# A two-block layer network on one core: the modulation products moved from TensorE to VectorE, half of them into the first feed-forward, and the filter adds from GpSimd to VectorE

## The chip, the cores and the metric

The kernel runs on one core of one Trainium2 chip. The metric is the device time of one execution in microseconds; lower is better. A core has a matrix engine (TensorE, "PE" in the rows, its weight loads "PEld"), a vector engine (VectorE, "DVE"), a scalar engine (ScalarE, "ACT"), GpSimd ("POOL") and a queue engine (SyncE, "SP") from which most transfers are issued.

## The reference, cut to what matters

Two hybrid layers (512 tokens, width 1024) are followed by two conditioned layers. A conditioned layer needs a modulation: six rows of 1024 numbers for the tokens and six for a 256-token context, each a product of a vector with a weight matrix of 1024 x 6144.

```python
mod_x = (jax.nn.silu(c) @ w_mod[i] + b_mod[i])[:, None, :]
mod_c = (jax.nn.silu(c_ctx) @ w_mod[i] + b_mod[i])[None, None, :]
sh1, sc1, ga1, sh2, sc2, ga2 = jnp.split(mod_x, 6, axis=-1)
csh1, csc1, cga1, csh2, csc2, cga2 = jnp.split(mod_c, 6, axis=-1)
hx = rmsnorm_2(x, g_pre_mix[i]) * (1.0 + sc1) + sh1
...
x = x + ga1 * rmsnorm_2(mix_x, g_post_mix[i])
if not last:
    ...        # the context's own mixer and feed-forward
fx = rmsnorm_2(x, g_pre_ffn[i]) * (1.0 + sc2) + sh2
x = x + ga2 * rmsnorm_2(conv_ffn(fx, ...), g_post_ffn[i])
```

In the last layer the context only gives keys and values, so of its six rows only the first two (csh1, csc1) are used. Each conditioned layer also has a long convolution whose filter is made by a small network of sines and then normalised by its sum of absolute values.

## The kernel before, in words

`block1` computes the two hybrid layers, `block2` the two conditioned layers. Everything is unrolled. Large products are done in three parts (`mm3`, L560 to L562) on weights that are first split in two (`split`: ScalarE rounds, L528, VectorE subtracts, L529).

The order of the work is written out by generators. `weave` takes several generators with a total each, and always advances the one that has done the smallest share of its total (a `yield` of 0.45 adds 0.45). For each hybrid layer `weave_hybrid` weaves the attention, the dense products (`mtile`: a 512 KB weight tile, 24 matmuls) and side streams: the modulation and, in layer 0, the filters (`prep`). The order on an engine is then settled when the program is built, from the order of the code and from the dependences, so an instruction may stand ahead of earlier code that is not ready.

The modulation (`modulation`) loops over 2 layers, 6 rows and 8 blocks of 128 input features, 96 steps in all. A step loads 128 x 1024 weights (512 KB), multiplies them on TensorE in four column groups of 256 by the two activated vectors (L1322; a profile shows each as two matmuls, 8 to a step) and adds the bank to a 128 x 256 accumulator on VectorE (L1324 for the first block, L1326 for the others). After 8 steps come bias and gain (L1331, L1332) and the way out to DRAM. Layer 0's 48 steps are woven into hybrid layer 0, layer 1's into hybrid layer 1. `mod_columns` and `mod_row` read the rows back later.

`filters` runs three times beside hybrid layer 0. For each block of 128 positions it multiplies (L1217), decays (L1218), takes the absolute value (L1219), adds it to a total on GpSimd (L1221), and after the last block adds the halves on GpSimd (L1222), sums over partitions on TensorE (L1224), takes the reciprocal (L1225), makes sums and differences on GpSimd (L1231) and scales them (L1232). All the blocks of a call are issued in one step.

`Ffn.run` is the feed-forward. For conditioned layer 0 (tokens and context together, 768 columns) it makes 22 hidden tiles by `up` and takes them in ten parts of mostly two; for each part but the last, `down` is called six times (4 token tiles, 2 context tiles), each time for two banks of 512 columns, which VectorE adds to an accumulator (L2077; the first part is copied by ScalarE). `down` takes its banks from a ring of four, `up` from a ring of two pairs.

Of the kernel before, what the change touches and what calls it, by code (L numbers as in the profile page):

```python
# [11 lines left out]
AF = mybir.ActivationFunctionType  # L12
# [4 lines left out]
P = 128  # L17
# [254 lines left out]
def drain(gen):  # L272
    for _ in gen:
        pass
# [156 lines left out]
class Net:  # L431
# [273 lines left out]
    def block1(self):  # L705
# [32 lines left out]
        for l in range(DEPTH):  # L738
            self.weave_hybrid(l, [(self.some(mod, T["modn"] if l == 0 else 96), T[f"m{l}"])] + ([(self.some(prep, T["prepn"]), T["p0"])] if l == 0 else [(prep, T["p1"])]))
# [464 lines left out]
    def filters(self, l, tag, banks):  # L1204
# [7 lines left out]
        for t in range(nt):  # L1212
# [85 lines left out]
    def modulation(self):  # L1298
# [7 lines left out]
        cs = self.new(KD, 32)  # L1306
        nc.vector.memset(cs, 0.0)
        nc.vector.tensor_scalar(cs[:, :, 0:2], t.rearrange("p (s k) -> p k s", s=2), 0.5, None, op0=ALU.mult)
        self.mod = {}
        ws, accs = self.ring(1024, 2), self.ring(256, 2)  # L1310
        yield 0.0
        for l in range(DEPTH):
            md = self.dram(f"mod_{l}", (2, 6 * D))
            self.mod[l] = md
            for r in range(6):
                acc = accs()
# [12 lines left out]
                w = ws(512)  # L1329
                nc.sync.dma_start(w, d["modbg"][l, r])  # L1330
# [897 lines left out]
```

## Time and profile before

| | |
|---|---|
| median of 3 runs | 2293.55 us (2291.92 to 2294.4) |
| the profiled execution, its own time | 2299.32 us |
| its span, first to last instruction | 2297.3 us, 31229 instructions |
| PE busy | 2193.8 us, 95% |
| DVE busy | 1418.7 us, 62% |
| ACT busy | 1015.2 us, 44% |
| POOL busy | 231.6 us, 10% |
| mean granted TensorE clock | 0.985 of 2.4 GHz |
| moved by DMA | 235.88 MB, mean 103 GB/s |

An engine's busy time is the union of its instructions' durations. The ends of matmuls are modelled, so a PE that is busy all the time need not be at its peak. The span is read in stages: hybrid layer 0 is woven from about 65 to 330 us, hybrid layer 1 from about 420 to 665 us, the main part of the first feed-forward lies at 1110 to 1610 us.

### The profile page before, as it was taken

Reading aid. Unit: us, or ns where it says so; the run is one execution under the profiler, and the core shown is the slowest. Engines: PE = TensorE matmul, PEld = TensorE weight load, DVE = VectorE, ACT = ScalarE, POOL = GpSimd, SP = SyncE. Lnnn points to the kernel's source line nnn. Section 1 sums busy time; section 2 is a strip of 40 time slices with the busy share of each in tenths; the row PEclk is TensorE's granted clock in tenths of the full one; section 3 lists DMA queues with packets and bytes.
Section 4 is the critical chain, followed back from the end, with each engine's and each line's share of the span. In section 5 each row is a group of like instructions: output and inputs, shape, how many; then the busy total and the mean of one; then the engine's idle time right before and its main releaser. Section 6 shows DMA issues by size and latency. Waiting matters only on the chain.

```text
span 2297.3 us, 31229 instructions
## 1 busy us (share of the span) xinstructions
PE 2193.8 (95%) x12119; PEld 1748.6 (76%) x12122; DVE 1418.7 (62%) x2498; ACT 1015.2 (44%) x1896; POOL 231.6 (10%) x388
## 2 busy tenths in 40 slices
PE   7989999999999988999999999999899999999997
PEld 6545678755577777788888888888677889888886
DVE  5665776347667466676655655665877666456556
ACT  4335355246336335765532332323455664333332
POOL 2052012112012110010000000000320000000001
PEclk9989999999999999999999999999999999999999
DMA  5566523355532122323211221212134131233321
GB/s 193 176 193 197 180 78 106 116 178 169 166 114 74 46 76 98 112 77 111 83 56 46 83 74 55 70 60 67 49 101 135 60 102 65 74 101 110 101 93 63
DMA packets 72596, 235.88 MB, mean 103 GB/s; under 512 B 9056, under 2 KB 11136, under 8 KB 72448
## 3 DMA queue, kind: packets, MB, share of 16 engines
q1 hardware_dynamic: 65392, 223.06, 30.0%
q10 hardware_dynamic: 7056, 10.83, 1.6%
q8 instruction: 95, 1.56, 0.3%
q14 instruction: 53, 0.43, 0.1%
HBM read 225.37 MB, written 8.49 MB: 102 GB/s over the span
## 4 chain that ended last, share of the span: by engine, by line
PE 61%; DVE 6%; ACT 3%; POOL 3%; DMA 2%; issue 1%; POOLq 0%; DVEq 0%; ACTq 0%
PE f L561 10%; PE f L560 10%; PE f L562 10%; PE b L560 8%; PE b L562 7%; PE b L561 7%; POOL small L570 2%; PE b L1942 2%; PE b L909 2%; DVE page L529 1%; PE f L1915 1%; PE b L908 1%; ACT page L528 1%; PE f L1916 1%; POOL small L569 1%
## 5 line engine op out<-in xcount | busy, mean ns | idle before, releaser
L528 ACT ACTIVATE page<-page 128x1024 fp32r<-128x1024 f32 (+7 forms) x472 | 393.4, 846 | 639.8 <-PE f L561 159.5
L529 DVE TENSOR_TENSOR page<-page,page 128x1024 fp32r<-128x1024 f32 (+7 forms) x472 | 452.4, 970 | 319.4 <-ACT page L528 295.7
L560 PE MATMUL f<-page,page 128*128 128x512 f32 (+2 forms) x1452 | 518.0, 359 | 7.5 <-ACT page L528 7.5
L561 PE MATMUL f<-page,page 128*128 128x512 f32 (+2 forms) x1444 | 518.3, 359 | 1.0 <-DVE page L529 1.0
L560 PE MATMUL b<-page,page 128*128 128x512 f32 (+3 forms) x1356 | 513.0, 379 | 5.3 <-ACT page L528 1.7
L562 PE MATMUL f<-page,page 128*128 128x512 f32 (+2 forms) x1452 | 516.8, 357 | 0.0
L561 PE MATMUL b<-page,page 128*128 128x512 f32 (+3 forms) x1354 | 501.4, 371 | 0.4 <-DVE page L529 0.4
L562 PE MATMUL b<-page,page 128*128 128x512 f32 (+3 forms) x1346 | 498.3, 371 | 2.2 <-DVE page L529 2.2
L560 PEld LDWEIGHTS f<-page,page 128*128 128x128 f32 x1452 | 273.5, 189 | 51.3 <-ACT page L528 10.8
L560 PEld LDWEIGHTS b<-page,page 128*128 128x128 f32 x1356 | 256.1, 189 | 66.0 <-issue 16.4
L562 PEld LDWEIGHTS f<-page,page 128*128 128x128 f32 x1452 | 273.8, 189 | 39.8 <-DVE page L529 1.5
L561 PEld LDWEIGHTS f<-page,page 128*128 128x128 f32 x1444 | 272.8, 189 | 40.0 <-DVE page L529 3.1
L561 PEld LDWEIGHTS b<-page,page 128*128 128x128 f32 x1354 | 256.4, 189 | 47.9 <-issue 9.3
L562 PEld LDWEIGHTS b<-page,page 128*128 128x128 f32 x1346 | 254.7, 189 | 45.9 <-issue 5.6
L2077 DVE TENSOR_TENSOR page<-b,page 128x512 f32<-128x512 f32 x148 | 100.5, 687 | 84.5 <-PE b L562 84.4
L1401 ACT ACTIVATE page<-f,page 128x512 f32<-128x512 f32 (+1 forms) x128 | 89.2, 697 | 119.0 <-PE f L562 118.8
L569 POOL TENSOR_SCALAR small<-small 128x1 f32<-128x1 f32 (+3 forms) x104 | 41.8, 402 | 866.0 <-DVE small L2088 359.1
L1402 DVE SCALAR_TENSOR_TENSOR page<-f,page,page 128x511 f32<-128x511 f32 (+1 forms) x128 | 84.0, 656 | 69.8 <-ACT page L1401 69.7
L1403 DVE SCALAR_TENSOR_TENSOR page<-f,page,page 128x511 f32<-128x511 f32 (+1 forms) x128 | 84.3, 659 | 3.7
L570 POOL TENSOR_TENSOR small<-small,nhalf 128x1 f32<-128x1 f32 (+3 forms) x104 | 84.0, 808 | 8.6
L1920 DVE TENSOR_REDUCE small<-f 128x1 f32<-128x768 f32 (+1 forms) x80 | 66.8, 845 | 21.5 <-PE f L1916 21.4
L1322 PE MATMUL b<-page,page 128*32 128x256 f32 x768 | 64.1, 396 | 7.1 <-DMA page<-w_mod 6.9
(300 smaller groups left out, 2472.0 us busy)
## 6 DMA issues: line engine op xcount, KB each, us to landing
page<-w_mod SPq DMA_DIRECT2D x96, 512.0 KB
page<-b_up SPq DMA_DIRECT2D x88, 512.0 KB
page<-b_dn SPq DMA_DIRECT2D x44, 512.0 KB
page<-b_wa SPq DMA_DIRECT2D x42, 512.0 KB
page<-b_wo SPq DMA_DIRECT2D x40, 512.0 KB
page<-b_wq SPq DMA_DIRECT2D x14, 512.0 KB
page<-b_wkvf SPq DMA_DIRECT2D x12, 512.0 KB
page<-b_wp SPq DMA_DIRECT2D x12, 512.0 KB
```

The costliest lines, as they stand in the source:

```text
L528: nc.scalar.activation(h, src, AF.Copy)
L529: nc.vector.tensor_tensor(l, src, h.bitcast(F32), op=ALU.subtract)
L560: first = nc.tensor.matmul(out, lhsT=ah, rhs=bh, start=start, stop=False, skip_group_check=skip)
L561: nc.tensor.matmul(out, lhsT=ah, rhs=bl, start=False, stop=False, skip_group_check=skip)
L562: nc.tensor.matmul(out, lhsT=al, rhs=bh, start=False, stop=stop, skip_group_check=skip)
L569: nc.gpsimd.tensor_scalar(r, ssq, 1.0 / dim, EPS, op0=ALU.mult, op1=ALU.add)
L570: nc.gpsimd.tensor_tensor(r, r, self.nhalf[:, :n], op=ALU.pow)
L1401: nc.scalar.activation(o, ps, AF.Identity, scale=taps[:, 1:2], bias=taps[:, 3:4])
L1402: nc.vector.scalar_tensor_tensor(o[:, 1:], ps[:, : n - 1], taps[:, 0:1], o[:, 1:], op0=ALU.mult, op1=ALU.add)
L1403: nc.vector.scalar_tensor_tensor(o[:, : n - 1], ps[:, 1:], taps[:, 2:3], o[:, : n - 1], op0=ALU.mult, op1=ALU.add)
L1920: nc.vector.tensor_reduce(mx, s, axis=AX.X, op=ALU.max, negate=True)
L2077: nc.vector.tensor_tensor(o, ps, o, op=ALU.add)
```

## The change

Three things change. First, the modulation's products leave TensorE: a step now loads 128 x 512 weights (256 KB, a ring of four), and VectorE multiplies them by one column of the activated vector as a scalar for each partition, once for the tokens and once for the context, and adds to an accumulator of 128 x 2 x 512. When eight blocks of both halves are through, `mod_sums` sums over the partitions on TensorE with a selection matrix that puts the two streams on rows 0 and 1, once for each 1024 columns and stream, a few steps late. There are now 96 steps a layer. Layer 0's are woven over both hybrid layers, 48 in each. Second, layer 1's 96 steps move into the first feed-forward, two ahead of each `down`, and from its third row on it leaves out the context, which is not used; `mod_columns` reads only what was written. Third, the filters' adds go from GpSimd to VectorE, and `filters` yields after each block instead of once. The totals of the weave change with it.

```diff
-            self.weave_hybrid(l, [(self.some(mod, T["modn"] if l == 0 else 96), T[f"m{l}"])] + ...
+            self.weave_hybrid(l, [(self.some(mod, 48 if l == 0 else 96), 50.0)] + ...
...
             if t:
-                (nc.vector if T["fse"] else nc.gpsimd).tensor_tensor(total, total, dec, op=ALU.add)
-        nc.gpsimd.tensor_tensor(r, total[:, :256], total[:, 256:], op=ALU.add)
+                nc.vector.tensor_tensor(total, total, dec, op=ALU.add)
+            yield 0.85
+        nc.vector.tensor_tensor(r, total[:, :256], total[:, 256:], op=ALU.add)
+        yield 0.25
...
-        yield 0.9 * nt + 0.5
+        yield 0.05 * nt + 0.25
...
-                (nc.vector if T["foe"] else nc.gpsimd).tensor_tensor(o[:, j], fb[:, t, :256], fb[:, t, 256:], op=op)
+                nc.vector.tensor_tensor(o[:, j], fb[:, t, :256], fb[:, t, 256:], op=op)
...
-        ws, accs = self.ring(1024, 2), self.ring(256, 2)
-                    nc.sync.dma_start(w, d["w_mod"][l, k, :, r * D : r * D + D])
-                    ps = self.pt(256)
-                    for j in range(4):
-                        nc.tensor.matmul(ps[32 * j : 32 * j + 32], lhsT=cs[:, k], rhs=w[:, 256 * j : 256 * j + 256], start=True, stop=True, tile_position=(0, 32 * j))
-                    if k == 0:
-                        nc.vector.tensor_copy(acc, ps)
-                    else:
-                        nc.vector.tensor_tensor(acc, ps, acc, op=ALU.add)
-                    if k < KD - 1:
-                        yield 0.45
...
+        yield from self.mod_layer(0, self.pt)
+
+    def mod_layer(self, l, banks):
+        nc, d = self.nc, self.d
+        md = self.dram(f"mod_{l}", (2, 6 * D))
+        self.mod[l] = md
+        ws, accs = self.ring(512, 4), self.ring(1024, 3)
+        late = None
+        for r in range(6):
+            n = 1 if l and r > 1 else 2
+            both = []
+            for h in range(2):
+                acc = accs(2, 512)
+                both.append(acc)
+                for k in range(KD):
+                    w = ws()
+                    nc.sync.dma_start(w, d["w_mod"][l, k, :, r * D + 512 * h : r * D + 512 * h + 512])
+                    for s in range(n):
+                        c = self.silu[:, 8 * s + k : 8 * s + k + 1]
+                        if k == 0:
+                            nc.vector.tensor_scalar(acc[:, s], w, c, None, op0=ALU.mult)
+                        else:
+                            nc.vector.scalar_tensor_tensor(acc[:, s], w, c, acc[:, s], op0=ALU.mult, op1=ALU.add)
+                    yield 0.5 * n
+                    if late and k == 2:
+                        self.mod_sums(md, l, *late, banks)
+                        late = None
+            late = r, n, both
+        self.mod_sums(md, l, *late, banks)
+        self.free(ws, accs)
+
+    def mod_sums(self, md, l, r, n, both, banks):
+        nc = self.nc
+        bg = self.raw(512)
+        nc.scalar.dma_start(bg, self.d["modbg"][l, r])
+        ps = banks()[:, :256]
+        for s in range(n):
+            for j in range(4):
+                src = both[j // 2][:, s, 256 * (j % 2) : 256 * (j % 2) + 256]
+                nc.tensor.matmul(ps[32 * j : 32 * j + 32], lhsT=self.sel[:, s], rhs=src, start=s == 0, stop=s == n - 1, tile_position=(0, 32 * j))
+        o = bg[:, :256]
+        nc.vector.tensor_tensor(o, ps, o, op=ALU.add)
+        nc.vector.tensor_tensor(o, o, bg[:, 256:], op=ALU.mult)
+        for s in range(n):
+            src = o.rearrange("(j q) n -> j q n", q=32)[:, s, :]
+            nc.sync.dma_start(md[s, r * D : r * D + D].rearrange("(j n) -> j n", j=4), src)
...
+        mod = net.mod_layer(1, self.pd) if both else iter(())
...
             for s in range(1 + both):
                 for t in range((NT, 2)[s]):
+                    if both:
+                        MARK("mod")
+                        for _ in zip(range(2), mod):
+                            pass
                     MARK(f"f{self.l} main")
                     self.down(p == 0, gs, ws, t, s)
+        drain(mod)
```

## Rows read from the trace of the kernel before

**Rows 1.** The page's first part: busy us (share of the span) xinstructions.

```profile
PE 2193.8 (95%) x12119; PEld 1748.6 (76%) x12122; DVE 1418.7 (62%) x2498; ACT 1015.2 (44%) x1896; POOL 231.6 (10%) x388
```

**Rows 2.** Busy time by stretch: stretch, length, engines (instructions), granted clock, DMA share, GB/s.

```profile
65.00:330.00 265.00, 250.84 (x1340) 157.83 (x1340) 173.84 (x402) 119.13 (x256) 55.59 (x93) 0.96 0.53 169
...
420.00:665.00 245.00, 235.92 (x1324) 152.29 (x1325) 142.00 (x363) 111.08 (x246) 29.25 (x63) 0.99 0.50 159
...
1110.00:1610.00 500.00, 500.00 (x2690) 433.09 (x2690) 292.84 (x386) 161.02 (x203) 1.04 (x2) 1.00 0.21 68
1610.00:1680.00 70.00, 58.02 (x257) 45.19 (x256) 57.57 (x105) 35.12 (x72) 24.58 (x30) 0.93 0.18 55
```

**Rows 3.** Modulation matmuls, layer 0 (65:330) then 1 (420:665): busy, mean ns | idle before.

```profile
L1322 PE MATMUL b<-page,page 128*32 128x256 f32 x384 | 31.6, 402 | 2.7 <-DMA page<-w_mod 2.5
...
L1322 PE MATMUL b<-page,page 128*32 128x256 f32 x384 | 32.5, 390 | 4.4 <-DMA page<-w_mod 4.4
```

**Rows 4.** Timeline of PE: one modulation step, start us and duration us.

```profile
441.80 0.64 PE L1322 MATMUL b<-page,page 128*32 128x256 f32 x8
```

**Rows 5.** Modulation on DVE: three groups of 65:330, then one of 420:665.

```profile
L1326 DVE TENSOR_TENSOR page<-b,page 128x256 f32<-128x256 f32 x42 | 17.7, 420 | 15.3 <-PE b L1322 14.9
...
L1332 DVE TENSOR_TENSOR page<-page,page 128x256 f32<-128x256 f32 x6 | 2.6, 434 | 0.0
...
L1324 DVE COPY page<-b 128x256 f32<-128x256 f32 x6 | 2.5, 422 | 6.4 <-PE b L1322 6.3
...
L1326 DVE TENSOR_TENSOR page<-b,page 128x256 f32<-128x256 f32 x42 | 17.7, 422 | 37.0 <-PE b L1322 36.5
```

**Rows 6.** Nearest DVE rows to the new operations, min/median/max ns or busy, mean ns.

```profile
L903 DVE SCALAR_TENSOR_TENSOR page<-page,page x15: 671/684/693, 212.7 to 648.0; 128x512 f32<-128x512 f32 x15
...
L1064 DVE TENSOR_SCALAR page<-page,small 128x512 f32<-128x512 f32 x4 | 1.9, 484 | 0.1
...
L607 DVE TENSOR_TENSOR page<-page,page 128x256 fp32r<-128x256 f32 x88 | 33.2, 419 | 2.7 <-ACT page L606 2.5
```

**Rows 7.** Filter adds on POOL in 65:330, and a wait behind them (total, times, longest).

```profile
L1231 POOL TENSOR_TENSOR page<-page 128x256 f32<-128x256 f32 x20 | 15.0, 775 | 7.6 <-DMA sd_1x<-page 7.6
L1221 POOL TENSOR_TENSOR page<-page,page 128x512 f32<-128x512 f32 x7 | 8.9, 1272 | 57.4 <-ACT page L1219 57.3
...
L1222 POOL TENSOR_TENSOR page<-page 128x256 f32<-128x256 f32 x3 | 2.8, 939 | 0.2
...
DVE page L1232 <- POOL page L1231: 6.8, 4, 3.6
```

**Rows 8.** Waits in 65:290: ScalarE for GpSimd.

```profile
ACT page L528 <- POOL page L953: 16.0, 11, 5.5
```

**Rows 9.** Timeline of DVE in the feed-forward, after an up and among the downs.

```profile
1249.48 0.69 DVE L2077 TENSOR_TENSOR page<-b,page 128x512 f32<-128x512 f32 x1 [0.67 <-PE b L562]
1250.84 0.69 DVE L2077 TENSOR_TENSOR page<-b,page 128x512 f32<-128x512 f32 x1 [0.67 <-PE b L562]
...
1307.29 1.23 DVE L529 TENSOR_TENSOR page<-page,page 128x1024 fp32r<-128x1024 f32 x1 [1.46 <-ACT page L528]
1308.43 0.48 DVE L1402 SCALAR_TENSOR_TENSOR page<-f,page,page 128x255 f32<-128x255 f32 x1
1308.82 0.68 DVE L2077 TENSOR_TENSOR page<-b,page 128x512 f32<-128x512 f32 x1
1309.42 0.47 DVE L1403 SCALAR_TENSOR_TENSOR page<-f,page,page 128x255 f32<-128x255 f32 x1
1309.93 0.96 DVE L2059 TENSOR_TENSOR page<-page,page 128x768 f32<-128x768 f32 x1
...
1311.80 0.96 DVE L529 TENSOR_TENSOR page<-page,page 128x768 fp32r<-128x768 f32 x1 [0.31 <-ACT page L528]
```

**Rows 10.** Waits in 1110:1610, and the modulation's transfers on the page.

```profile
DVE page L2077 <- PE b L562: 44.7, 52, 1.4
...
page<-w_mod SPq DMA_DIRECT2D x96, 512.0 KB
```

More of the change, by code (lines that the diff above doesn't have):

```diff
@@ L738, in block1 @@
         for l in range(DEPTH):
-            self.weave_hybrid(l, [(self.some(mod, T["modn"] if l == 0 else 96), T[f"m{l}"])] + ([(self.some(prep, T["prepn"]), T["p0"])] if l == 0 else [(prep, T["p1"])]))
+            self.weave_hybrid(l, [(self.some(mod, 48 if l == 0 else 96), 50.0)] + ([(self.some(prep, T["prepn"]), T["p0"])] if l == 0 else [(prep, T["p1"])]))
             if l == DEPTH - 1:
@@ L1220, in filters @@
             if t:
-                (nc.vector if T["fse"] else nc.gpsimd).tensor_tensor(total, total, dec, op=ALU.add)
-        nc.gpsimd.tensor_tensor(r, total[:, :256], total[:, 256:], op=ALU.add)
+                nc.vector.tensor_tensor(total, total, dec, op=ALU.add)
+            yield 0.85
+        nc.vector.tensor_tensor(r, total[:, :256], total[:, 256:], op=ALU.add)
+        yield 0.25
+        MARK("filters")
         ps = self.pt(256)
@@ L1305, in modulation @@
         nc.vector.scalar_tensor_tensor(t, t, 1.0, cc, op0=ALU.add, op1=ALU.mult)
-        cs = self.new(KD, 32)
-        nc.vector.memset(cs, 0.0)
-        nc.vector.tensor_scalar(cs[:, :, 0:2], t.rearrange("p (s k) -> p k s", s=2), 0.5, None, op0=ALU.mult)
+        cs, sel = self.new(16), self.new(2, 32)
+        nc.vector.memset(sel, 0.0)
+        for s in range(2):
+            nc.vector.memset(sel[:, s, s : s + 1], 1.0)
+        nc.vector.tensor_scalar(cs, t, 0.5, None, op0=ALU.mult)
         self.mod = {}
-        ws, accs = self.ring(1024, 2), self.ring(256, 2)
+        self.silu, self.sel = cs, sel
@@ L1311, in modulation @@
         yield 0.0
[L1312 to L1316, printed above, removed]
+        yield from self.mod_layer(0, self.pt)
[11 more added lines that the diff above has]
+                both.append(acc)
@@ L1327, in modulation @@
-                    if k < KD - 1:
-                        yield 0.45
-                w = ws(512)
-                nc.sync.dma_start(w, d["modbg"][l, r])
-                nc.vector.tensor_tensor(acc, acc, w[:, :256], op=ALU.add)
-                nc.vector.tensor_tensor(acc, acc, w[:, 256:], op=ALU.mult)
-                for s in range(2):
-                    src = acc.rearrange("(j q) n -> j q n", q=32)[:, s, :]
-                    nc.sync.dma_start(md[s, r * D : r * D + D].rearrange("(j n) -> j n", j=4), src)
@@ L1336, in modulation @@
-                yield 0.45
-        self.free(cs, ws, accs)
-        yield 0.0
+                    nc.sync.dma_start(w, d["w_mod"][l, k, :, r * D + 512 * h : r * D + 512 * h + 512])
[5 more added lines that the diff above has]
+                            nc.vector.scalar_tensor_tensor(acc[:, s], w, c, acc[:, s], op0=ALU.mult, op1=ALU.add)
@@ L1348, in mod_columns @@
         for s in range(2):
-            rows = self.wa()[:48, :P]
-            nc.sync.dma_start(rows, self.mod[l][s].rearrange("(k p) -> k p", p=P))
-            pt = self.b[s][:, :48]
-            nc.tensor.transpose(pt, rows, self.ident[:48, :48])
+            n = 16 if l and s else 48
+            rows = self.wa()[:n, :P]
+            nc.sync.dma_start(rows, self.mod[l][s, : n * P].rearrange("(k p) -> k p", p=P))
+            pt = self.b[s][:, :n]
+            nc.tensor.transpose(pt, rows, self.ident[:n, :n])
             m = self.new(48)
-            nc.scalar.activation(m, pt, AF.Copy)
-            for j, o in ((0, 8), (1, 32)):
+            nc.scalar.activation(m[:, :n], pt, AF.Copy)
+            for j, o in ((0, 8), (1, 32))[: n // 16]:
                 g = vec[:, 8 * j : 8 * j + 8]
```

## The prediction

> **What bounds the kernel now.** I read the page's busy shares first, then busy time by stretch, then the groups by line inside the stretches that the change touches, then waits and timelines.
>
> PE is busy 95% of the span and DVE 62% [rows 1]. These are averages over unlike stages. In the feed-forward PE has no idle microsecond in 500, and DVE works 292.84, 59% [rows 2]. In the two weaves PE is busy 250.84 of 265 and 235.92 of 245, but its weight loads only 157.83 and 152.29 against 433.09 of 500 in the feed-forward [rows 2]. Part of that is work of another shape, part may be PE held up where the model of matmul ends does not show it. So PE sets the pace in the feed-forward; in the weaves it is the busiest engine, and DVE is second with 173.84 (66%) and 142.00 (58%) [rows 2]. The reader should see that DVE has 207 us to spare in the feed-forward, 91 in weave 0 and 103 in weave 1.
>
> **What leaves TensorE.** The modulation's matmuls cover 31.6 us of PE in weave 0 and 32.5 in weave 1, with 2.7 and 4.4 us of idle PE before them, nearly all for their transfers [rows 3]: 34.3 and 36.9 us. In their place come 12 sums over partitions. Eight logged matmuls of this shape take 0.64 us [rows 4]; a sum over both streams has sixteen, 1.28 us, over one stream eight, 0.64. Three sums fall in each weave, 3.8 us. So PE's share alone would give 34.3 - 3.8 = 30.5 us in weave 0 and 33.1 in weave 1, and weave lengths of 234.5 and 211.9.
>
> **What comes to VectorE in the weaves.** No row shows the new operation with these operands. The nearest is a scalar_tensor_tensor of 128x512 f32 from SBUF to SBUF, 684 ns (671 to 693) [rows 6]; the first block of eight is a tensor_scalar of 128x512, 484 ns [rows 6]. Their spreads are small, so I take the medians. Layer 0 has 6 rows x 2 halves x 8 blocks x 2 streams = 192 operations, 24 of them first: 168 x 0.684 + 24 x 0.484 = 126.5 us, 63.3 in each weave. Away go 17.7 us of adds from the bank, 2.5 of copies [rows 5], and three of the six pairs of bias and gain, 2.6 (L1332 has 2.6 for six, its partner is alike) [rows 5]: 22.8 a weave.
>
> The filter adds, all in weave 0, go from GpSimd to DVE: 20 of 128x256, 7 of 128x512 and 3 of 128x256 [rows 7]. By the 419 ns of a 128x256 subtraction and the 684 ns above [rows 6] they cost 8.4 + 4.8 + 1.3 = 14.5 us of DVE. They free 26.7 us of GpSimd and a wait of 6.8 us that DVE had behind it [rows 7]. I give the finer yields nothing: they only move the same work, and PE has the dense products to cover them. If the cover fails they could win or lose about that 6.8.
>
> DVE's load is then 173.8 - 22.8 + 63.3 + 14.5 = 228.8 us in weave 0 and 142.0 - 22.8 + 63.3 = 182.5 in weave 1.
>
> **What of PE's gain is left.** In weave 0 DVE would have to be busy 228.8 of 234.5, 98%. It is late next: its own waits move from the bank of the modulation (14.9 us of L1326 [rows 5]) to the attention's chains. The fullest stretch of any length that I found has DVE at 57.57 of 70, 82% [rows 2]. At 82% weave 0 takes 278.3, 13.3 longer; at 98% it gains the whole 30.5. The new operations need only their weights and wait for no other engine, so they fill holes that the attention leaves, which speaks for more than 82%; I take 90%: 254.2, a gain of 10.8. In weave 1 the same 82% gives 222.0 and PE's bound is 211.9; I take the middle, 217, a gain of 28.0.
>
> **The first feed-forward.** Layer 1 has 32 steps of two streams and 64 of one: 128 operations, 16 of them first, 112 x 0.684 + 16 x 0.484 = 84.3 us, and six pairs of bias and gain, 5.2. DVE goes from 292.8 to 382.3 of about 505, 76%, under the 82% seen. PE gets two sums of 1.28 and four of 0.64, 5.1 us, all on the path, since PE has no idle time. The lower bound is 5.1. For the upper one the operations run exactly where the code puts them, between the downs (the fourth rival), 61.4 us. They need not: in the timeline an add of a down stands between two operations of the up before it, at 1308.82 [rows 9], so the order is filled where an operand is ready, and with four weight buffers the new operations can run ahead into holes of the ups. I take 12: the 5.1 and about 1 us of held-up PE at each sum, whose bias and gain now borrow one of the two raw weight buffers.
>
> The weight transfers keep their bytes. In the weaves the modulation's bytes halve at the same number of issues (48 of 256 KB for 48 of 512 KB [rows 10]), in the feed-forward SP issues 96 more. There DMA is busy 21% for 34 MB at 68 GB/s [rows 2]; 25 MB more make about 37%. I count nothing: the up's weights are fetched well before use. Should SP stand behind a modulation buffer that DVE frees late, the up's weights come late, and that is the fourth rival again.
>
> Sum: -10.8 - 28.0 + 12 = -26.8 us. The profiled execution took 2299.32 us, 2.0 more than its span, so it would take 2272.5. It is 5.8 above the median of the runs, 2293.55; from that, 2267.
>
> **A rule against it.** Two POOL operations of the filters and DVE's L1232 delay each other in the weave by semaphores [rows 7], and ScalarE waits 16.0 us for POOL's triangle masks [rows 8]. The Trainium skill (SBUF — State Buffer, SBUF: two separate sides) says that a DVE operation with two SBUF inputs and a GpSimd operation that reads SBUF exclude each other, the later one waiting for the whole instruction. The old modulation adds read a bank, the new ones read SBUF twice; by the rule they would hold up GpSimd, and by the row alone they cost only themselves. This is the fifth rival.
>
> **The rivals.**
> 1. The forecast: DVE eats part of PE's gain in weave 0, little in weave 1. 2267, own range 2250 to 2284. For it: DVE's shares after the change lie between what rows show and full. Chance 0.46.
> 2. DVE holds nothing up: both weaves at PE's bound, only the sums in the feed-forward, -30.5 - 33.1 + 5.1 = -58.5, 2235. For it: the operations are free of other engines; against it: 98% of DVE in weave 0. Chance 0.15.
> 3. DVE becomes the bound of both weaves at 82%: +13.3 - 23.0 + 12 = +2.3, 2296. For it: attention is a chain of short DVE operations, each of which may stand behind one of 0.68 us. Chance 0.19, of it 0.14 within 0.2%.
> 4. Slower: DVE falls behind PE in the downs. A turn has twelve banks, 1.36 us apart [rows 9], 16.3 us of PE. DVE adds them in 12 x 0.69 = 8.3 us and idles half the time for PE (44.7 us in all [rows 10]). Two streams put 24 operations of 0.684 into a turn, 16.4 us: 24.7, so 8.4 us late in each of 32/12 = 2.7 turns, 22.4. One stream: 8.3 + 8.2, 0.2 late in 5.3 turns, 1.1. Ahead of each turn DVE still has 1.23 + 0.48 + 0.47 + 0.96 + 0.96 = 4.1 us of the up's work [rows 9], 32.8 in 8 turns. With the sums 61.4; -38.8 + 61.4 = +22.6, 2316. It decides once the feed-forward grows by more than 38.8 + 4.6 = 43.4 us. Against it: operations can be moved up. Chance 0.15.
> 5. The exclusion of GpSimd: 63 POOL instructions remain in each weave (93 less the 30 adds, and 63 [rows 2]). The 84 two-input operations fill 57.5 of 254 us, 23%; a POOL instruction that meets one waits 0.34 us on average: 63 x 0.23 x 0.34 = 4.9 us a weave if all of it lies on the path, -17.0 in all, 2277. Chance 0.05.
>
> **How the numbers follow.** 0.2%, 4.6 us, is about what a measurement of this kernel can tell from no change. Faster by more: rivals 1, 2 and 5, 0.66. Within: 0.14. Slower: the rest of 3 and all of 4, 0.20. The predicted time is the forecast's. The range, 2240 to 2306, leaves out about half of rival 2 and most of rival 4; it holds rival 3.
>
> **What would show each step.** PE busy in weave 0 and 1 together should fall by about 56 us, with 160 logged small matmuls in the whole trace in place of 768. The new DVE group should show about 280 operations of 128x512 near 684 ns; 900 or more would mean another price. DVE's share should stand near 90% in weave 0 and 84% in weave 1, and the stage from 420 to 665 should shrink more than the first. PE should stay without idle time in the feed-forward, which grows by 5 to 20 us; waits of PE for L2077 or for weight splits there would be rival 4. POOL's affine_select rows longer than now would be rival 5. The prediction is wrong if PE's gain in weave 1 does not come, or if the feed-forward grows by over 40 us.

## The result and the profile after

The median went from 2293.98 us (4 runs, 2291.92 to 2297.15) to 2262.57 us (4 runs, 2259.54 to 2265.52): a ratio of 0.9858 [0.9845, 0.9872], 31.4 us faster. The forecast was 2267. The two profiled executions, 2299.32 and 2259.54 us, lie 39.8 us apart, 8.4 more than the medians, since the one of before is slower and the one of after faster than its median. A stage length below comes from one execution each; the last feed-forward, which no kernel here touches, comes out between 385.2 and 389.1 us in all of them, so a difference of 4 us in one stage is not read as an effect.

The first part of the page after, to be held against [rows 1]:

```profile
PE 2147.3 (95%) x11514; PEld 1739.1 (77%) x11514; DVE 1581.9 (70%) x2753; ACT 1018.1 (45%) x1898; POOL 222.2 (10%) x358
```

PE has 46.5 us less to do and DVE 163.2 more, yet the shares are 95% and 70%: they show that work went over, and nothing of what it was worth.

Busy time by stretch, after: weave 0, weave 1, the main part of the first feed-forward, columns as in [rows 2].

```profile
65.00:308.00 243.00, 222.64 (x1002) 153.54 (x1002) 221.02 (x474) 123.81 (x261) 40.24 (x64) 0.97 0.39 127
400.00:624.00 224.00, 214.50 (x1039) 152.00 (x1039) 169.14 (x395) 108.98 (x246) 35.22 (x66) 1.00 0.32 102
1065.00:1576.00 511.00, 509.89 (x2780) 437.32 (x2779) 371.98 (x518) 161.51 (x203) 1.04 (x2) 1.00 0.35 117
```

DVE works 91% of weave 0 (forecast 90), 76% of weave 1 (forecast 84) and 73% of the feed-forward (forecast 76). PE lost 28.2 and 21.4 us of busy time in the weaves, 49.6 together (forecast 56). In the feed-forward PE has 1.1 us without work. So the loads fell about where the prediction put them, DVE's in weave 1 below it.

The new operations, by line, after (name and shape, count, min/median/max ns, first and last start):

```profile
L1342 DVE SCALAR_TENSOR_TENSOR page<-page,page,page x248: 730/743/1214, 49.1 to 1475.2; 128x512 f32<-128x512 f32 x124
...
L1340 DVE TENSOR_SCALAR page<-page,page x40: 471/478/742, 48.3 to 1466.0; 128x512 f32<-128x512 f32 x40
...
L1359 PE MATMUL b<-page,page x160: 379/379/636, 132.9 to 1568.6; 128*32 128x256 f32 x160
```

With 32 more of L1342 under another name there are 280 multiply-adds; they take 743 ns, not the 684 of [rows 6]. 160 small matmuls stand where there were 768 [rows 3].

Where the time went is read from stage borders. Each is the first transpose of a norm (L594) behind the stage. The timelines of PE, before and then after (start us, duration us), give these ends of hybrid 0 and hybrid 1 and the two ends of the first feed-forward:

```profile
366.19 1.04 PE L594 MATMUL f<-ident,page 128*128 128x128 f32 x8
...
702.87 1.03 PE L594 MATMUL f<-ident,page 128*128 128x128 f32 x8
...
1041.09 0.60 PE L594 MATMUL b<-ident,page 128*128 128x128 f32 x4
...
1635.09 0.38 PE L594 MATMUL f<-ident,page 128*128 128x128 f32 x2
```

```profile
344.54 0.38 PE L594 MATMUL f<-ident,page 128*128 128x128 f32 x2
...
663.03 1.03 PE L594 MATMUL f<-ident,page 128*128 128x128 f32 x8
...
996.05 0.60 PE L594 MATMUL b<-ident,page 128*128 128x128 f32 x4
...
1601.77 0.38 PE L594 MATMUL f<-ident,page 128*128 128x128 f32 x2
```

Differences of such borders, for both kernels and all the experiments, in us:

| kernel | hybrid 0 | hybrid 1 | cond. 0, mixing | first feed-forward | cond. 1, mixing |
|---|---|---|---|---|---|
| before | 366.2 | 336.7 | 338.2 | 594.0 | 274.5 |
| after | 344.5 | 318.5 | 333.0 | 605.8 | 270.8 |
| filters_back | 358.7 | 322.2 | 332.2 | 606.3 | 271.7 |
| filters_alone | 362.7 | 337.2 | 339.2 | 594.1 | 274.3 |
| both_in_weaves | 404.8 | 338.9 | 337.8 | 596.2 | 276.6 |
| two_streams | 347.9 | 319.9 | 332.1 | 606.4 | 273.1 |
| no_products_before | 342.5 | 309.7 | 341.4 | 594.8 | 274.9 |
| moved_on_pe | 345.7 | 313.5 | 331.3 | 640.2 | 273.0 |
| no_stt_layer0 | 360.5 | 308.9 | 331.8 | 609.6 | 274.0 |
| no_stt_layer1 | 345.1 | 319.4 | 332.4 | 606.1 | 271.1 |
| no_mod_layer0 | 347.4 | 312.5 | 334.5 | 614.3 | 275.3 |
| wide | 364.2 | 328.5 | 347.9 | 606.7 | 280.2 |
| const_scalar | 348.3 | 318.9 | 333.4 | 605.5 | 272.7 |
| ctx_on_pool | 375.4 | 344.9 | 337.7 | 609.4 | 276.3 |

After against before: hybrid 0 gained 21.7 us (forecast 10.8), hybrid 1 18.2 (forecast 28.0), together 39.9 (forecast 38.8). The first feed-forward grew by 11.8 (forecast 12). The mixing ahead of it fell by 5.2 and the one behind it by 3.7, which was not forecast. Some 4 us of the 5.2 and of the 11.8 are the same work on the other side of a border: between the two ends of the first feed-forward stand 72 matmuls of 128x256 into a bank before and 106 after, and the mixing has 34 fewer (384 and 350). One of their three lines, in the feed-forward before and then after:

```profile
L562 PE MATMUL b<-page,page 128*128 128x256 f32 x24 | 6.8, 285 | 0.0
```

```profile
L562 PE MATMUL b<-page,page 128*128 128x256 f32 x36 | 10.2, 282 | 0.0
```

(The 4 us are an estimate: 34 of them at the 0.12 us that lie between their starts.) So the sum of the weaves was right and its halves were not: the experiments ask why.

Three more readings. In the feed-forward DVE still waits for PE's banks (waits, after: us, times, longest us):

```profile
DVE page L2105 <- PE b L562: 27.5, 34, 1.4
...
DVE page L1342 <- DMA page<-w_mod: 4.6, 5, 2.5
```

The 44.7 us of [rows 10] shrank to 27.5: part of the multiply-adds ran inside that wait. They wait 4.6 us for their own weights, and PE waits 0.6 us for the end of their sums (L1361, next row).

PE's groups of 1065:1576 after, then those of the same part of the stage before (1100:1600; busy us, mean ns | idle us before):

```profile
L560 PE MATMUL b<-page,page 128*128 128x512 f32 (+1 forms) x234 | 91.0, 389 | 0.8 <-DVE page L1361 0.6
...
L1359 PE MATMUL b<-page,page 128*32 128x256 f32 x64 | 4.7, 388 | 0.0
```

```profile
L560 PE MATMUL b<-page,page 128*128 128x512 f32 (+1 forms) x228 | 87.4, 383 | 0.0
```

The sums over partitions take 4.7 us (forecast 5.1), and the downs' matmuls are a few ns longer each.

GpSimd's triangle masks, weave 0 after and then before (busy us, mean ns | idle before):

```profile
L978 POOL TENSOR_SCALAR_AFFINE_SELECT page<-page 128x128 f32<-128x128 f32 x16 | 10.0, 632 | 29.5 <-ACT page L977 29.4
L953 POOL TENSOR_SCALAR_AFFINE_SELECT page<-page 128x128 f32<-128x128 f32 x16 | 8.4, 524 | 81.0 <-DMA page<-b_wa 50.5 <-DVE page L952 30.5
```

```profile
L978 POOL TENSOR_SCALAR_AFFINE_SELECT page<-page 128x128 f32<-128x128 f32 x16 | 6.5, 412 | 25.7 <-ACT page L977 25.7
L953 POOL TENSOR_SCALAR_AFFINE_SELECT page<-page 128x128 f32<-128x128 f32 x16 | 5.3, 331 | 20.8 <-DVE page L952 20.7
```

In the mean they grew from 412 to 632 and from 331 to 524 ns, the sign that the prediction named for its fifth rival. All of POOL's work in weave 0 other than the filters went from 55.59 - 26.7 = 28.9 us [rows 2, 7] to 40.24: 11.3 us more (1.3 of them one instruction more), where that rival counted 4.9.

That the multiply-adds do most of it can be seen in no_mod_layer0 (below), the kernel after without layer 0's multiply-adds and their loads. L953 in weave 0 (count, min/median/max ns), after and then without them:

```profile
L953 POOL TENSOR_SCALAR_AFFINE_SELECT page<-page x16: 292/455/1047, 108.3 to 193.4; 128x128 f32<-128x128 f32 x16
```

```profile
L953 POOL TENSOR_SCALAR_AFFINE_SELECT page<-page x16: 288/295/1272, 110.9 to 194.7; 128x128 f32<-128x128 f32 x16
```

The median goes from 455 back to 295 (292 before); L978's goes from 528 to 388 (316 before), so a part of L978's growth is not theirs. A multiply-add and the mask that met it, after (start us, us):

```profile
191.94 0.74 DVE L1342 SCALAR_TENSOR_TENSOR page<-page,page,page 128x512 f32<-128x512 f32 x1
...
192.09 0.74 POOL L953 TENSOR_SCALAR_AFFINE_SELECT page<-page 128x128 f32<-128x128 f32 x1 [3.81 <-DVE page L952]
```

The mask begins 0.15 us behind the multiply-add and ends 0.15 us behind it, 0.74 us long where the shortest take 0.29.

### The profile page after: what moved, and what is told of

It is laid out like the page before. It is cut to its first block, busy times and chain, and to the rows that moved or that the text cites. A ratio compares the mean times of both kernels' runs of the same rounds, so it can differ in the third digit from the quotient of the medians.

```text
span 2257.8 us, 30406 instructions
## 1 busy us (share of the span) xinstructions
PE 2147.3 (95%) x11514; PEld 1739.1 (77%) x11514; DVE 1581.9 (70%) x2753; ACT 1018.1 (45%) x1898; POOL 222.2 (10%) x358
## 4 chain that ended last, share of the span: by engine, by line
PE 71%; DVE 8%; ACT 5%; POOL 4%; issue 2%; DMA 2%; DVEq 0%; POOLq 0%; ACTq 0%; SPq 0%
PE f L561 11%; PE f L560 10%; PE f L562 10%; PE b L560 9%; PE b L561 9%; PE b L562 9%; POOL small L570 2%; DVE page L529 2%; PE b L1970 2%; PE b L909 1%; ACT page L528 1%; PE b L908 1%; POOL small L569 1%; PE f L1943 1%; PE f L1031 1%
## 5 line engine op out<-in xcount | busy, mean ns | idle before, releaser
L528 ACT ACTIVATE page<-page 128x1024 fp32r<-128x1024 f32 (+6 forms) x472 | 393.3, 846 | 594.5 <-PE f L561 139.7
L529 DVE TENSOR_TENSOR page<-page,page 128x1024 fp32r<-128x1024 f32 (+6 forms) x472 | 449.3, 964 | 267.6 <-ACT page L528 252.0
L561 PEld LDWEIGHTS f<-page,page 128*128 128x128 f32 x1452 | 274.9, 189 | 44.8 <-DVE page L529 7.9
L562 PEld LDWEIGHTS f<-page,page 128*128 128x128 f32 x1452 | 274.5, 189 | 40.0 <-DVE page L529 1.2
L1342 DVE SCALAR_TENSOR_TENSOR page<-page,page,page 128x512 f32<-128x512 f32 x248 | 179.6, 750 | 5.9 <-DMA page<-w_mod 5.0
```

What stands on the lines that cost most here:

```text
L528: nc.scalar.activation(h, src, AF.Copy)
L529: nc.vector.tensor_tensor(l, src, h.bitcast(F32), op=ALU.subtract)
L561: nc.tensor.matmul(out, lhsT=ah, rhs=bl, start=False, stop=False, skip_group_check=skip)
L562: nc.tensor.matmul(out, lhsT=al, rhs=bh, start=False, stop=stop, skip_group_check=skip)
L1342: nc.vector.scalar_tensor_tensor(acc[:, s], w, c, acc[:, s], op0=ALU.mult, op1=ALU.add)
```

## The experiments

Each ratio is against the kernel before on the same chip; after has 0.9858 on that scale, and 0.1% is 2.3 us. A short diff is against after unless it says before.

**filters_back and filters_alone: what are the filters' adds worth?** The first puts them back on GpSimd with the single yield; the second makes only that part of the change.

```diff
-                nc.vector.tensor_tensor(total, total, dec, op=ALU.add)
-            yield 0.85
-        nc.vector.tensor_tensor(r, total[:, :256], total[:, 256:], op=ALU.add)
-        yield 0.25
-        MARK("filters")
+                (nc.vector if T["fse"] else nc.gpsimd).tensor_tensor(total, total, dec, op=ALU.add)
+        nc.gpsimd.tensor_tensor(r, total[:, :256], total[:, 256:], op=ALU.add)
...
-        yield 0.05 * nt + 0.25
+        yield 0.9 * nt + 0.5
...
-                nc.vector.tensor_tensor(o[:, j], fb[:, t, :256], fb[:, t, 256:], op=op)
+                (nc.vector if T["foe"] else nc.gpsimd).tensor_tensor(o[:, j], fb[:, t, :256], fb[:, t, 256:], op=op)
```

> The kernel after, with the filters' adds on GpSimd and one yield a call again. Theory 1 (the gain is PE's products, the filters are worth nothing): within 7 us of the kernel after, 2256 to 2269 us. Theory 2 (the first hybrid layer gained 21 us where 11 were forecast, because the filters' wait for GpSimd and the PE holes behind it went): about 10 us above the kernel after, 2273.

> The kernel before, with only the filters' adds on VectorE and the finer yields. Theory 1: within 0.3% of before, at best the 6.8 us of the wait. Theory 2: 10 us faster than before, 2284.

filters_back took 2278.57 us, 0.9912 [0.9898, 0.9925], 12 us slower than after (0.54% of 2298); its hybrid 0 is 14 us longer. filters_alone took 2299.6, 1.0005 [0.9996, 1.0015]: nothing. So the filters' part is worth nothing by itself and 12 us beside the products on VectorE; neither theory had both. GpSimd's groups of filters_back in 65:330, and PE's waits there in 65:318:

```profile
L1231 POOL TENSOR_TENSOR page<-page 128x256 f32<-128x256 f32 x20 | 17.9, 921 | 4.0 <-DVE page L1218 3.8
L1221 POOL TENSOR_TENSOR page<-page,page 128x512 f32<-128x512 f32 x7 | 10.9, 1561 | 3.6 <-ACT page L1219 3.5
```

```profile
PE b L1224 <- POOL page L1222: 7.3, 3, 3.8
...
PE f L908 <- POOL page L978: 4.6, 2, 3.1
```

The adds grew from 775 and 1272 ns [rows 7] to 921 and 1561, and PE waits 7.3 us for the filters' halves and 4.6 for the masks queued among them; together 11.9, near the 14. In weave 0 of after it waits 0.5 us for L978 and not for the filters' halves. Which share belongs to the finer yields was not tried apart, so it is not shown that the engine alone makes the 12 us.

**both_in_weaves: does VectorE limit if it gets more?** All of layer 0 goes into hybrid 0, layer 1 into hybrid 1, as before, but on VectorE.

```diff
-            self.weave_hybrid(l, [(self.some(mod, 48 if l == 0 else 96), 50.0)] + ...
+            self.weave_hybrid(l, [(self.some(mod, 96 if l == 0 else 200), (100.0, 67.0)[l])] + ...
...
         yield from self.mod_layer(0, self.pt)
+        yield from self.mod_layer(1, self.pt)
...
-        mod = net.mod_layer(1, self.pd) if both else iter(())
+        mod = iter(())
```

> The kernel after, with layer 1's modulation back in hybrid layer 1 and layer 0's all in hybrid layer 0, still on VectorE. Theory 1 (VectorE, 91% busy in the first weave, is what limits it now): its load there rises by some 70 us, at 91% the first weave grows by about 77, the second stays, the feed-forward gives back 10: some 2330 us, slower than before. Rival (VectorE still has room, PE is the bound): 10 us below the kernel after, 2253.

2344.2 us, 1.0198 [1.0184, 1.0212]: 78 us slower than after (3.4%). Hybrid 0 grew by 60, hybrid 1 by 20 (it was expected to stay), the feed-forward fell by 9.6. Weave 0 by stretch, and PE's longest wait in it:

```profile
65.00:368.00 303.00, 246.64 (x1046) 166.14 (x1047) 276.18 (x567) 123.30 (x258) 37.13 (x63) 0.90 0.46 141
```

```profile
PE b L562 <- DVE page L529: 15.2, 7, 5.4
```

DVE is again busy 91% (276.18 of 303), and now the stretch grows with its work: this is the price of the change without the move. PE, which waits 15.2 us for split weights, also gets a mean granted clock of 0.90 in place of 0.97, so part of the stretch ran at 1.2 GHz. 91% is thus about as full as DVE gets over this whole weave, though parts of it reach 97 and 98% in after (48.55 of 50 and 43.95 of 45, shown at no_stt_layer0). What 55 more microseconds of DVE work cost, 60 us, does not follow from what the first 59 cost.

**two_streams and no_stt_layer1: do the products cost anything in the feed-forward?** The first keeps the unused context of layer 1, 64 operations more; the second cuts layer 1's multiply-adds to 32 columns.

```diff
-            n = 1 if l and r > 1 else 2
+            n = 2
```

```diff
+                        elif l:
+                            nc.vector.scalar_tensor_tensor(acc[:, s, :32], w[:, :32], c, acc[:, s, :32], op0=ALU.mult, op1=ALU.add)
```

> The kernel after, with the context's stream kept in all rows of layer 1: 64 more VectorE operations in the feed-forward, 47 us of VectorE, and four more single sums, 2.6 us of PE. Theory 1 (the operations fill holes): 3 to 10 us above the kernel after, 2266 to 2273. The fourth rival (operations run between the downs, each two-stream turn 8.4 us late): 5.3 more late turns, 45 us, 2308.

> The kernel after, with layer 1's multiply-adds on VectorE cut to 32 of 512 columns (the modulation of layer 1 is wrong). Theory 1: of the feed-forward's growth of some 12 us the sums' 5 stay, 3 to 8 us below the kernel after. The fourth rival (VectorE late in the downs): all but the sums goes, and the waits of PE in the feed-forward vanish with it.

two_streams took 2271.67 us, 0.9881 [0.9864, 0.9899], its feed-forward 606.4; no_stt_layer1 2264.32 us, 0.9847 [0.9833, 0.9862], its feed-forward 606.1. After has 605.8. The stretch 1065:1576 of the one, then of the other:

```profile
1065.00:1576.00 511.00, 511.00 (x2829) 439.39 (x2828) 408.84 (x587) 162.48 (x207) 1.04 (x2) 1.00 0.37 115
```

```profile
1065.00:1576.00 511.00, 510.25 (x2790) 438.27 (x2789) 320.48 (x516) 159.98 (x202) 1.04 (x2) 1.00 0.36 117
```

DVE's work goes from 320 over 372 to 409 us of 511 and the stage does not move: the products are free there, and the fourth rival is out. The 0.23% by which two_streams is slower than after lies in no single stage, and the intervals overlap. The 3 to 8 us that no_stt_layer1 was expected to win did not come: its feed-forward is no shorter, so what the stage grew by is not the products.

**no_products_before: what was PE's work worth in the weaves?** Before, without seven of eight blocks' matmuls and adds; the loads stay.

```diff
-                    ps = self.pt(256)
-                    for j in range(4):
-                        nc.tensor.matmul(ps[32 * j : 32 * j + 32], lhsT=cs[:, k], rhs=w[...], start=True, stop=True, ...)
                     if k == 0:
+                        ps = self.pt(256)
+                        for j in range(4):
+                            nc.tensor.matmul(ps[32 * j : 32 * j + 32], lhsT=cs[:, k], rhs=w[...], start=True, stop=True, ...)
                         nc.vector.tensor_copy(acc, ps)
-                    else:
-                        nc.vector.tensor_tensor(acc, ps, acc, op=ALU.add)
```

> The kernel before, with the modulation's matmuls and adds left out for 7 of 8 blocks (weights still loaded, so the modulation is wrong). Theory 1 (in the weaves PE's products lay on the path with their whole rows): 7/8 of 34.3 + 36.9 us gone, 62 us below before. Rival (PE had slack in the weaves that its busy time hides): less than 40 us.

2260.54 us against 2299.56, 0.9834 [0.9818, 0.9851]: 39 us. Hybrid 0 fell by 23.7 and hybrid 1 by 27.0. It leaves PE 48 small matmuls a weave, as many as after's three sums, so this is what taking the products from PE gives there with the loads and the filters as before. The prediction had 30.5 and 33.1 for it. Its ends of hybrid 0 and hybrid 1:

```profile
342.51 1.04 PE L594 MATMUL f<-ident,page 128*128 128x128 f32 x8
...
652.23 0.38 PE L594 MATMUL f<-ident,page 128*128 128x128 f32 x2
```

Its profiled execution, 2253.91 us, is its fastest, so its stages add up to more than the 39 us of the medians. Weave 0 by stretch:

```profile
65.00:310.00 245.00, 224.00 (x1013) 153.58 (x1013) 162.80 (x365) 121.74 (x260) 57.11 (x94) 0.97 0.57 187
```

PE shows 224.00 us busy of 245, just as after does with 222.64 of 243, with DVE at 66% here and at 91% there.

**moved_on_pe: is it the engine or the place?** Before, with the products on PE, but layer 0 over both weaves and layer 1 in the feed-forward.

```diff
-            self.weave_hybrid(l, [(self.some(mod, T["modn"] if l == 0 else 96), T[f"m{l}"])] + ...
+            self.weave_hybrid(l, [(self.some(mod, 24 if l == 0 else 96), 11.25)] + ...
...
+        mod = net.mod_layer(1, self.pd) if both else iter(())
...
+                    if both:
+                        next(mod, None)
```

> The kernel before, with the modulation's products left on TensorE, but layer 0's spread over both hybrid layers and layer 1's moved into the first feed-forward, a step ahead of each down. Theory 1 (the engine is what counts): some 36 us less in the weaves, 31 or more in the feed-forward where PE has no idle time: within 5 us of before. Rival (the place is what counts): 15 us or more below before.

2296.48 us, 0.9992 [0.9982, 1.0003]: no change. The hybrids gain 20.5 and 23.2, the feed-forward loses 46.2. Its ends of hybrid 0 and hybrid 1, and the two ends of the first feed-forward:

```profile
345.72 1.04 PE L594 MATMUL f<-ident,page 128*128 128x128 f32 x8
...
659.24 1.03 PE L594 MATMUL f<-ident,page 128*128 128x128 f32 x8
...
990.47 0.66 PE L594 MATMUL b<-ident,page 128*128 128x128 f32 x4
...
1630.70 0.38 PE L594 MATMUL f<-ident,page 128*128 128x128 f32 x2
```

So the place alone gives nothing, and VectorE in the weaves alone loses 46 us (both_in_weaves): the gain needs both. The stages say where each counts. PE still has 192 small matmuls, 16 us, in each hybrid, and the hybrids are 3.2 and 3.8 us longer than those without the products (no_products_before). Against them after's hybrids, with this half on VectorE, are 1.2 us shorter and 5.0 us longer, though after has the filters' adds off GpSimd; with them on GpSimd on both sides, VectorE's half makes the hybrids 13.0 and 8.7 us longer than PE's half (filters_back against moved_on_pe). So in the weaves the move of half the products is worth all that the change gains there, and the change of engine pays in the feed-forward, 11.8 us in place of 46.2. A kernel that leaves layer 0's half on TensorE in each weave and takes only layer 1's products to VectorE was not tried.

**no_stt_layer0 and no_mod_layer0: does VectorE's work cost time in the weaves?** The first leaves out layer 0's 168 multiply-adds and keeps their loads, the second leaves out the loads too.

```diff
-                        else:
+                        elif l:
                             nc.vector.scalar_tensor_tensor(acc[:, s], w, c, acc[:, s], op0=ALU.mult, op1=ALU.add)
```

```diff
-                    w = ws()
-                    nc.sync.dma_start(w, d["w_mod"][l, k, :, r * D + 512 * h : r * D + 512 * h + 512])
+                    if k == 0 or l:
+                        w = ws()
+                        nc.sync.dma_start(w, d["w_mod"][l, k, :, r * D + 512 * h : r * D + 512 * h + 512])
...
-                        else:
+                        elif l:
```

> The kernel after, with layer 0's 168 multiply-adds on VectorE left out (weights loaded, first blocks and sums kept). Theory 1 (VectorE gives back part of PE's gain in the weaves): both weaves go to PE's bound, about 9 us less in the first hybrid layer and 15 in the second, 24 us below the kernel after. Rival (VectorE has room; what is left is attention's own chain): less than 5 us.

> The kernel after, with layer 0's multiply-adds left out as in the run before and their weight transfers too (7 of 8 blocks). Theory 1 (without the multiply-adds to hold them back, the transfers rushed in and delayed the first hybrid layer by 16 us): the first hybrid layer at or below the 344 us of the kernel after, the whole at most 2250. Rival (a matter of the order of instructions, not of transfers): the first hybrid layer stays near 360, the whole near 2275.

no_stt_layer0 took 2275.99 us, 0.9898 [0.9883, 0.9913]: less work, and 9 us slower than after. Hybrid 1 fell by 9.6, but hybrid 0 grew by 16. Three stretches of it, then of after:

```profile
20.00:65.00 45.00, 38.74 (x209) 34.52 (x207) 22.16 (x47) 21.10 (x52) 10.84 (x24) 1.00 0.79 248
65.00:110.00 45.00, 38.86 (x158) 27.90 (x159) 31.33 (x58) 13.89 (x27) 0.00 (x0) 0.92 0.78 254
110.00:160.00 50.00, 36.33 (x119) 21.70 (x120) 31.10 (x59) 22.70 (x46) 10.86 (x21) 0.80 0.60 191
```

```profile
20.00:65.00 45.00, 39.21 (x211) 34.95 (x209) 27.18 (x59) 20.17 (x50) 10.70 (x24) 1.00 0.47 144
65.00:110.00 45.00, 39.12 (x159) 27.18 (x160) 43.95 (x79) 20.39 (x39) 1.12 (x4) 0.94 0.39 129
110.00:160.00 50.00, 43.17 (x159) 25.77 (x158) 48.55 (x88) 24.35 (x48) 12.20 (x22) 0.92 0.45 158
```

Nothing reads the weights, so no buffer holds the loads back: DMA's share is 0.79 and 0.78 where after has 0.47 and 0.39, and the attention's own weights come late. PE's wait for b_ukv in weave 0, 1.0 us in after, is here:

```profile
PE f L868 <- DMA page<-b_ukv: 5.8, 1, 5.8
```

Behind it PE is less busy and the granted clock of 110:160 is 0.80, after's 0.92. no_mod_layer0 takes that rush away: hybrid 0 is 347.4, so the rush was 13 of the 16. But it is no shorter than after's 344.5, with 52 us less DVE work in the weave, 168.46 in place of 221.02:

```profile
65.00:308.00 243.00, 223.55 (x1005) 154.80 (x1005) 168.46 (x385) 121.93 (x261) 33.26 (x63) 0.96 0.25 80
```

Of the expectation, 344 or less and at most 2250 in all, neither came: VectorE's products cost weave 0 nothing that a stage reading shows. In hybrid 1, where the other half of layer 0's products fell away, it is 6.0 shorter than after, no_stt_layer0 9.6. In all it took 2270.49 us, 0.9878 [0.9864, 0.9892], slower than after; 8.5 us of that lie in the feed-forward and 4.5 in the mixing behind it, which were not edited, and why is open.

**const_scalar and wide: the price of one operation, and fewer of them.** The first gives the multiply-adds a constant in place of the column of c; the second takes 1024 columns a step, half as many operations, and was meant as an improvement.

```diff
-                            nc.vector.scalar_tensor_tensor(acc[:, s], w, c, acc[:, s], op0=ALU.mult, op1=ALU.add)
+                            nc.vector.scalar_tensor_tensor(acc[:, s], w, 0.5, acc[:, s], op0=ALU.mult, op1=ALU.add)
```

```diff
-        ws, accs = self.ring(512, 4), self.ring(1024, 3)
+        ws, accs = self.ring(1024, 2), self.ring(2048, 2)
...
-            for h in range(2):
-                acc = accs(2, 512)
...
+            both = accs(2, D)
+            for acc in (both,):
```

> The kernel after, with a constant in place of the scalar of each partition in the multiply-adds (the modulation is wrong). Theory 1 (the 59 ns over the forecast row are the price of a scalar read for each partition): a multiply-add takes about 684 ns, 5 us less VectorE in each weave. Rival (the price is that of these buffers): 743 stays. The time: 0 to 8 us below the kernel after.

> The kernel after, with 1024 columns a step instead of 512: half as many VectorE operations and 512 KB a transfer, for the same products. A multiply-add of 512 columns takes 743 ns, of which 533 are the columns; 140 fixed parts of some 0.21 us go, 9 us in each weave. Theory 1 (VectorE, 91% busy, limits the first weave): 5 to 12 us below the kernel after, 2252. Rival (VectorE limits nothing now): within 4 us.

const_scalar took 2265.24 us, 0.9851 [0.9837, 0.9866], as after. Its line, and the group in wide:

```profile
L1342 DVE SCALAR_TENSOR_TENSOR page<-page,page x248: 672/684/1215, 51.2 to 1480.2; 128x512 f32<-128x512 f32 x124
```

```profile
L1340 DVE SCALAR_TENSOR_TENSOR page<-page,page,page 128x1024 f32<-128x1024 f32 x140 | 178.6, 1286 | 19.3 <-DMA page<-w_mod 19.1
```

684 ns is the row that the prediction used; the scalar of each partition is the 59 ns on top. Without them 280 operations are 16.5 us shorter and no time is won. wide does save DVE time (1286 ns for what takes two of 743), but took 2314.38 us, 1.0068 [1.0055, 1.0082], 48 us slower than after. Two weight buffers let DVE wait 19.1 us for weights, and hybrid 0 and 1 grew by 20 and 10; but the mixing of both conditioned layers grew too, by 15 and 9, without a modulation step in it; some 4 us of the 15 are the 34 matmuls that after has behind that border and wide ahead of it. Where the larger buffers push other ones is a guess; the cause is open.

**ctx_on_pool: GpSimd as a third engine.** In layer 0 ScalarE multiplies the context's product in place and GpSimd adds it. (`place` may try 600 times to find room, 60 in after.)

```diff
+                        if s and not l:
+                            p = w if k else acc[:, s]
+                            nc.scalar.activation(p, w, AF.Copy, scale=c)
+                            if k:
+                                nc.gpsimd.tensor_tensor(acc[:, s], acc[:, s], p, op=ALU.add)
```

> The kernel after, with the context's stream of layer 0 multiplied by ScalarE in place and added by GpSimd: 31 us of VectorE less in each weave, 42 adds of 128x512 more on GpSimd. Theory 1 (VectorE's load limits the first weave, GpSimd has room): 5 to 10 us below the kernel after. The fifth rival (a GpSimd operation and a two-input VectorE operation hold each other up): GpSimd's adds well over 1.29 us, multiply-adds over 743 ns, masks later; 5 to 20 us above the kernel after.

2328.78 us, 1.0136 [1.0122, 1.0149], 64 us slower than after; hybrid 0 +31, hybrid 1 +26. Groups of 65:330:

```profile
L1343 POOL TENSOR_TENSOR page<-page,page 128x512 f32<-128x512 f32 x37 | 53.8, 1453 | 51.9 <-ACT page L1341 44.8 <-PE b L877 5.8
L1347 DVE SCALAR_TENSOR_TENSOR page<-page,page,page 128x512 f32<-128x512 f32 x37 | 36.9, 997 | 4.2 <-DMA page<-w_mod 3.8
...
L1093 DVE TENSOR_SCALAR page<-page,small 128x256 f32<-128x256 f32 x16 | 12.1, 815 | 0.0
```

With GpSimd adding, the multiply-add takes 997 ns in the mean, and even L1093, a DVE operation with one tensor input, 815. The same line in weave 0 of after:

```profile
L1093 DVE TENSOR_SCALAR page<-page,small 128x256 f32<-128x256 f32 x16 | 4.5, 346 | 0.0
```

In the whole run 20 of L1093's 32 operations overlap none of GpSimd's adds and take 341 to 353 ns; of the 12 that do, nine take 671 to 1421. PE waits for L1093 in turn (7.2 us). So the two engines lengthen each other's operations.

## Why the prediction was right, and where it was not

**Direction and sum.** Forecast 2267, measured 2262.57. The weaves gave 39.9 us for 38.8, the feed-forward took 11.8 for 12. That products taken from PE shorten the weaves is shown by no_products_before (39 us), and that neither the place nor the engine does it alone by the pair moved_on_pe (no change) and both_in_weaves (2% slower). But the terms behind the two sums were off and cancelled, so that they came out this near is luck. The working also put the gain of the weaves down to PE's whole row; the hybrids gain as much, 43.7 us, when half of it leaves, and VectorE is needed for the half that goes into the feed-forward (moved_on_pe).

**The split of the weaves.** Two terms were off and cancelled. "PE's share alone would give 30.5 us in weave 0 and 33.1 in weave 1" was too large: no_products_before gives 23.7 and 27.0, 50.7 in place of 63.6. That the busy row counted time that the attention's waits would have filled is argued; what the runs show is that 16 us of the products left on PE in each hybrid cost 3 to 4 us (moved_on_pe). And what VectorE gives back, 19.7 and 5.1 in the forecast, was nothing in weave 0 (no_mod_layer0 is no shorter without the products) and 6 to 10 us in weave 1 (no_mod_layer0, no_stt_layer0). By subtraction, 50.7 less 2 and 9, the differences between after and no_products_before, is 39.9, where the working had 63.6 less 24.8. So the sign that weave 1 would shrink more than weave 0 did not come.

**Why the fuller weave was the cheaper one.** Six kernels with unlike work on PE and DVE (after, no_products_before, moved_on_pe, no_mod_layer0, two_streams, const_scalar) have a hybrid 0 of 342.5 to 348.3 us. Something else than PE's or DVE's load ends it there; that it is the attention's chain is only argued. In hybrid 1 the four kernels without VectorE products there (no_products_before, moved_on_pe, no_stt_layer0, no_mod_layer0) stand at 308.9 to 313.5 and those with after's full products (after, two_streams, no_stt_layer1) at 318.5 to 319.9, though DVE is busy only 76%. So a share of 90% told neither the loss in the one nor the absence of it in the other. That DVE does limit at 91% when more comes is shown by both_in_weaves, the third rival's mechanism with more load than the change puts there.

**The price of a multiply-add.** 743 ns, not 684. The step took L903 as the nearest row; the difference is the scalar operand (const_scalar). It adds 59 ns x 280 = 16.5 us of DVE, and moved no time.

**The feed-forward.** +11.8 for 12, and only in part for the reasons given. The products cost nothing there (no_stt_layer1, two_streams), as argued from the add that stood inside an up, and the sums take 4.7 us of PE for 5.1. The rest of the 12 was PE held up for about 1 us at each of six sums (5.1 and 6 are 11, not 12): PE waits 0.6 us for them in all. In its place some 4 us are the mixing's matmuls that came over the border, and the last 2 to 3 are what is left; the downs' matmuls are a few ns longer each, and why is open. The fourth rival is refuted: at 409 of 511 us DVE still holds nothing up.

**The filters at nothing.** Right by themselves (filters_alone), wrong in this change: adds and yields together are worth 12 us (filters_back). The step priced each edit against the trace of before, in which GpSimd's adds met fewer DVE operations with two SBUF inputs. The fifth rival's mechanism fits, at a place that the prediction did not look at: it counted the 63 POOL instructions that stay and not the 30 that leave. The masks show it (455 and 295 ns), and so do ctx_on_pool's 743 to 997. The Trainium skill (SBUF — State Buffer, SBUF: two separate sides) says of a DVE operation with two SBUF inputs and a GpSimd operation that reads SBUF that the later of the two waits for the whole instruction of the other. The trace agrees: the mask shown above ends 0.15 us behind the multiply-add that it met. How much of the filters' 12 us is this mechanism and how much the old single yield is not shown. The longer masks (POOL's 11.3 us) cost little: ScalarE waits 12.6 us for them where [rows 8] has 16.0.

## What to carry to other kernels

An engine's busy share does not price its work: leave the work out, in one run with its loads and in one without, and see what the stage does; here 30.5 and 33.1 us of busy and waiting PE were worth 23.7 and 27.0, and 52 us of DVE at 91% nothing. Work that waits for no other engine fits on a second engine beside a matmul stage that has no idle time: 84 us of it, by the forecast's row, lengthened this one by no more than a reading of a stage tells. So a move into such a stage and a change of engine can be worth 31 us together when each alone is worth nothing or less. Ask of each part of the work whether it needs both: here the half that stayed in the weaves did not need the other engine. Price edits in the company of the other edits: two that touch GpSimd and VectorE at once are not the sum of their parts.

## What the runs showed of the hardware that was not expected

- A scalar_tensor_tensor of 128x512 f32 takes 684 ns with a constant and 743 with a scalar for each partition from SBUF.
- A GpSimd mask of 128x128 that takes 0.29 us at its shortest took 0.74 beside a multiply-add of VectorE and ended 0.15 us behind it.
- A DVE operation with one tensor input in SBUF is longer beside GpSimd's adds too: L1093 takes up to 1421 ns there, and 341 to 353 where it meets none (ctx_on_pool).
- Work that reads a weight ring also paces its transfers. Without it the same loads took DMA's share from 0.47 to 0.79, delayed another stream's weights, and hybrid 0 became 16 us longer with less to compute; without the transfers too (no_mod_layer0) 13 of the 16 went.
- Where PE waited more the granted clock fell with it: 0.90 in weave 0 of both_in_weaves and 0.80 in a stretch of no_stt_layer0, each a mean of stretches at 2.4 and 1.2 GHz, which adds to the waits themselves.
